# Transposing the first branch's h and three groups of q, k by VectorE and DRAM instead of TensorE

## The chip, the cores and the metric

The program runs on one core of one Trainium2 chip. The metric is the device time of one execution in microseconds (us), the median of three runs. A core has TensorE (matrix products and, with an identity matrix as one operand, transposes; results go to the PSUM banks), VectorE (DVE), ScalarE (ACT), GpSimd (POOL), and SyncE (SP), which here issues nearly all DMAs. Each engine takes its own instructions in order and waits on semaphores for the others. All DMAs run on the same 16 DMA engines.

## The reference

A layer for 512 tokens with 1024 channels: a feed-forward block, then two branches that read the same normalized tokens u, then a second feed-forward block. All is float32. What matters here is the middle:

```python
z = u @ w_mix + b_mix                       # q_m,k_m,v_m,o_m, i,f gates, q_f,k_f,v_f, f_f, g_a,g_b
h_m = mlstm_chunkwise(q_m, k_m, v_m, i_m, f_m)                  # 4 heads of 256 channels
y_a = sigmoid(o_m) * rms_norm(h_m, mlstm_norm_g)                # the first branch, 512 x 1024
y_b = forgetting_attention(q_f, k_f, v_f, f_f, q_g, k_g)        # 16 heads of 64, q and k rms-normed
merged = sigmoid(g_a) * (y_a @ w_branch_a) + sigmoid(g_b) * (y_b @ w_branch_b)
x = x + g2 * (merged @ w_out)               # g2 etc. come from silu(c) @ w_ada + b_ada
```

The inputs' gains and biases are larger than usual, so products are taken in three float32r passes (below).

## The kernel before, in words

Every large product is split: an operand is kept as a high part in float32r and the rest as a low part, and each product of 128 x 128 weights with 512 columns is three matmuls (`mm3`, lines 127 to 129). A weight chunk arrives in a buffer `raw` (three of them, `raw`, line 92), ScalarE rounds it to `wh` (line 102), VectorE subtracts to get `wl` (line 104), four buffers each.

The stage that the change touches lies between about 470 us and 830 us of the span. Tokens lie in four blocks of 128 (`tb`). A value can lie token-major (partition = token) or channel-major (partition = channel).

- `mlstm_h(h)` makes the first branch's output of one of four heads token-major: for each token block, products into PSUM, a division into `hn` (line 1107), squares on ScalarE (line 1109); then a reciprocal root over the four blocks, four multiplications by VectorE (line 1115) and four stores to a DRAM tile `h_d` (line 1116). Two token blocks share one buffer of the tag `bc`, four buffers, which the broadcast rows of later heads use too.
- `fox_qkv(g)` makes q and k of four attention heads at a time, g = 0 to 3, token-major: 256 channels of q and 256 of k in one tile `tk` per token block (tag `tok`, four buffers). When the last chunk is in, `done` adds the bias (line 1127), then squares, sums, a reciprocal root and a multiplication by it (line 1147). Then it makes v.
- `fox_t(p)` turns the q and k of one pair of heads channel-major: four TensorE transposes of 128 x 128 for q and four for k (line 1202) into a PSUM bank, from which ScalarE (lines 1207 and 1211) and VectorE (line 1209) write the gained high and low parts `fq`, `fk` and `klz`. There are eight pairs, two to a group.
- `fox_s`, `fox_p`, `fox_o` are the scores, the softmax with the transposes of its result (line 1259), and the product with v, for one head each. `fox_s` loads a row A of `A_d` spread over the partitions (line 1219).
- `y_a(m)`, m = 0 to 7, is the output gate of 128 channels: a product with `w_mix`, a tanh (line 1309), a load of h from `h_d` as `ht` (line 1311, tag `tok`), four TensorE transposes (line 1314), a scaling by ScalarE into `ya` (line 1316) and a product by VectorE (line 1317). From m = 4 on each half of it also takes one step of `ada_row`: 128 rows of `w_ada` are loaded through `raw` and added up, scaled, by VectorE (line 304).

`run` writes the order: the attention's heads go through n = 0 to 17, and between their parts `advance(fill, k)` takes k steps of a generator that holds half chunks of the next group's `fox_qkv`, some gates (`gate`, whose result is stored at line 1335), and, from n = 12, `y_a`. `fox_t(1)` stands at n = 1, `fox_t(2)` at n = 3, and so on to `fox_t(6)` and `fox_t(7)` at n = 11. This written order is a priority. When the program is built, a planner in the framework takes, engine by engine, the first instruction in that order whose operands and buffers are free by its own modelled durations, so that an instruction may move ahead of others: the loads of four `ht` leave SP together, as soon as buffers of `tok` come free. On the chip each engine's order is then fixed.

Of the kernel before, what the change touches and what calls it, by code (L numbers as in the profile page):

```python
# [11 lines left out]
F32 = mybir.dt.float32  # L12
# [35 lines left out]
class Layer:  # L48
    def __init__(self, tc, es, A, out, dbg=None):
        self.tc, self.nc, self.es, self.A, self.out = tc, tc.nc, es, A, out  # L50
        self.dbg = dbg or {}
        pool = lambda name, **k: es.enter_context(tc.tile_pool(name=name, **k))
        self.cp = pool("const", bufs=1)
        self.up = pool("u", bufs=1)
        self.xp = pool("x", bufs=1)
        self.wp = pool("w", bufs=4)
        self.sp = pool("small", bufs=4)
        self.pg = pool("pg", bufs=4, space=PSUM)
        self.pt = pool("pt", bufs=4, space=PSUM)
# [3 lines left out]
        self.due = []  # L63
        self.free = self.pin = lambda i: i

# [223 lines left out]
    def ada_row(self, v, new, new_row, bank):  # L289
# [800 lines left out]
    def mlstm_h(self, h, ip):  # L1090
        nc, sp = self.nc, self.sp
        (Wh, Wl), (vh, vl) = self.W[h], self.vt[h]
        ss = sp.tile([P, NT], F32, name=self.nm("hs"), tag="hs", bufs=2)
        hs = []
        for tb in range(NT):
            if tb % 2 == 0:
                h2 = ip.tile([P, 2, 256], F32, name=self.nm("hn"), tag="bc", bufs=4)
            ps = self.tbank()
            for sb in range(tb + 1):
# [14 lines left out]
        for tb in range(NT):  # L1114
            nc.vector.tensor_scalar(hs[tb], hs[tb], r[:, tb:tb + 1], None, op0=MUL)
            nc.sync.dma_start(self.h_d[tb * P:(tb + 1) * P, h * 256:(h + 1) * 256], hs[tb])


    def fox_qkv(self, g, ip):
# [25 lines left out]
        for tb in range(NT):  # L1145
            t3 = tok[tb].rearrange("p (h d) -> p h d", h=8)
            nc.vector.tensor_tensor(t3, t3, r[:, tb * 8:(tb + 1) * 8].unsqueeze(2).to_broadcast([P, 8, 64]), op=MUL)
        if g == 3:
            self.fx[g] = tok, self.fx[g]
            return  # L1150
# [14 lines left out]
        def mkv(ch):  # L1165
# [7 lines left out]
            return make  # L1173
        self.fx[g] = (tok, vts[0])
        if len(gs) > 1:
            self.fx[3] = vts[1]
        if g:
# [6 lines left out]
    def fox_t(self, p, ap):  # L1184
# [13 lines left out]
        for i, R in ((0, R_FQ), (1, R_FK)):  # L1198
            c = i * 256 + pr * P
            b = self.tbank()  # L1200
            for tb in range(NT):
                nc.tensor.transpose(b[:, tb * P:(tb + 1) * P], tok[tb][:, c:c + P], self.ident)
            gc = self.colA[:, R + p:R + p + 1]
# [90 lines left out]


    def y_a(self, m, ap, ip):
        nc = self.nc
        def step():
            if m >= NK // 2:
                self.tick()  # L1300
# [10 lines left out]
        nc.sync.dma_start(ht, self.h_d[:, m * P:(m + 1) * P].rearrange("(b p) n -> p b n", p=P))  # L1311
        b = self.tbank()
        for tb in range(NT):
            nc.tensor.transpose(b[:, tb * P:(tb + 1) * P], ht[:, tb, :], self.ident)
        ya = ap.tile([P, T], F32, name=self.nm("ya"), tag="qk", bufs=16)
        nc.scalar.activation(ya, b, AF.Copy, scale=self.hmg[:, m:m + 1])
        nc.vector.scalar_tensor_tensor(ya, th, 1.0, ya, op0=ADD, op1=MUL)
        self.ya[m] = ya
        step()
        yield  # L1320
# [42 lines left out]
    def run(self):  # L1363
# [3 lines left out]
        self.h_d = self.dp.tile([T, D], F32, name="h_d")  # L1367
        self.v0_d = [self.dp.tile([P, 256], F32, name=f"v0_d{tb}") for tb in range(NT)]
        self.g_d = [self.dp.tile([P, T], F32, name=f"g_d{i}") for i in range(2 * NK)]

# [145 lines left out]
        with tc.tile_pool(name="att", bufs=1) as ip:  # L1516
# [17 lines left out]
            self.vt, self.W, self.fx, self.qkt, self.S = [None] * 4, {}, {}, {}, {}  # L1534
            def advance(gen, n):
                for _ in range(n):
                    next(gen, None)
            advance(self.v_mlstm(0, ip, ip), 99)
# [13 lines left out]
            for n in range(18):  # L1552
# [18 lines left out]
            advance(fill, 99)  # L1571
            for m in range(NK):
                self.dump(f"ya_{m}", self.ya[m])
# [94 lines left out]
```

## Time and profile before

| | |
|---|---|
| median of three runs | 1321.18 us (1319.3 to 1321.39) |
| the profiled execution, its own time | 1319.86 us |
| its span | 1318.1 us, 17796 instructions |
| granted TensorE clock | 1.00 of full speed |
| TensorE busy | 1303.3 us, 99% |
| VectorE busy | 953.4 us, 72% |
| ScalarE busy | 630.3 us, 48% |
| DMA | 254.18 MB in 204488 packets |

The profiled execution takes 1.8 us more than its span, and lies 1.3 us below the median. "PE" is TensorE's matmuls (transposes among them), "PEld" its weight loads. Matmuls overlap, so that the duration of one is longer than its pitch; a row of several, xN, of the chain view gives the time that they take on the path. An entry "A <- B" in a list of waits says that A waited and B ended the wait.

### The profile page before, as it was taken

How to read it: one execution, taken by the hardware profiler on the slowest of the kernel's cores; microseconds unless marked ns; L12 is line 12 of the kernel's file. 1: busy time of each engine (PE TensorE's matmuls, PEld its weight loads, DVE VectorE, ACT ScalarE, POOL GpSimd, SP SyncE). 2: the span in 40 equal slices, each digit the busy share in tenths (PEclk: the TensorE clock that was granted, in tenths of full speed). 3: DMA queues.
4: the chain of work that ended last, by engine and by line, in shares of the span. 5: the costliest groups of instructions: out<-in, count | busy, mean ns of one | idle time of the engine just before them, and what ended most of it. 6: DMA issues, size and time to landing. Idle time of an engine off the chain costs nothing.

```text
span 1318.1 us, 17796 instructions
## 1 busy us (share of the span) xinstructions
PE 1303.3 (99%) x6345; PEld 1092.2 (83%) x6345; DVE 953.4 (72%) x1735; ACT 630.3 (48%) x1056; POOL 36.9 (3%) x57
## 2 busy tenths in 40 slices
PE   7999999999999999999999999999999999999998
PEld 6788888888899888888888788878898888888887
DVE  6877777578788687887887778777567557635787
ACT  5623232355476555566566666334372223223642
POOL 1000000000010101000000000003000000000000
PEclk9999999999999999999999999999999999999999
DMA  9998978465845434533343536777539767634574
GB/s 287 278 316 291 326 265 278 149 198 166 299 120 145 117 104 130 155 106 113 89 121 76 171 98 194 215 255 234 185 104 325 255 232 278 220 104 133 171 263 149
DMA packets 204488, 254.18 MB, mean 193 GB/s; under 512 B 15008, under 2 KB 146752, under 8 KB 204400
## 3 DMA queue, kind: packets, MB, share of 16 engines
q1 hardware_dynamic: 204016, 252.98, 60.1%
q8 instruction: 50, 0.82, 0.3%
q14 instruction: 38, 0.31, 0.1%
q0 software_dynamic: 320, 0.06, 0.0%
q10 hardware_dynamic: 64, 0.02, 0.0%
HBM read 217.28 MB, written 35.72 MB: 192 GB/s over the span
## 4 chain that ended last, share of the span: by engine, by line
PE 86%; DMA 4%; DVE 4%; ACT 3%; SPq 1%; issue 1%; DVEq 0%; ACTq 0%
PE g L129 22%; PE g L127 22%; PE g L128 22%; PE t L127 4%; PE t L129 4%; PE t L128 4%; DMA raw<-in_w_branch_a_dram 2%; PE g L909 1%; PE t L1289 1%; PE t L1259 1%; DMA raw<-in_w_ada_dram 1%; PE t L1230 1%; DVE wl L104 1%; PE t L1231 1%; DMA raw<-in_w_branch_b_dram 1%
## 5 line engine op out<-in xcount | busy, mean ns | idle before, releaser
L102 ACT ACTIVATE wh<-raw 128x1024 fp32r<-128x1024 f32 (+2 forms) x246 | 249.2, 1017 | 378.0 <-PE g L128 118.5
L104 DVE TENSOR_TENSOR wl<-raw,wh 128x1024 fp32r<-128x1024 f32 (+2 forms) x246 | 287.2, 1170 | 163.9 <-ACT wh L102 141.9
L127 PE MATMUL g<-uh,wh 128*128 128x512 f32 (+1 forms) x880 | 341.0, 387 | 0.0
L128 PE MATMUL g<-ul,wh 128*128 128x512 f32 (+1 forms) x880 | 339.5, 386 | 0.4 <-DVE ul L268 0.4
L129 PE MATMUL g<-uh,wl 128*128 128x512 f32 (+1 forms) x880 | 339.6, 386 | 0.0
L129 PEld LDWEIGHTS g<-uh,wl 128*128 128x128 f32 x880 | 165.3, 188 | 33.6
L128 PEld LDWEIGHTS g<-ul,wh 128*128 128x128 f32 x880 | 165.4, 188 | 33.2 <-DVE ul L268 0.6
L127 PEld LDWEIGHTS g<-uh,wh 128*128 128x128 f32 x880 | 165.3, 188 | 32.6 <-issue 0.6
L304 DVE SCALAR_TENSOR_TENSOR acc<-raw,ccol,acc 128x512 f32<-128x512 f32 (+1 forms) x70 | 66.8, 975 | 45.0 <-DMA raw<-in_w_ada_dram 44.9
L127 PE MATMUL g<-wh,uh 128*128 128x512 f32 (+1 forms) x256 | 97.4, 381 | 0.0
L129 PE MATMUL g<-wh,ul 128*128 128x512 f32 (+1 forms) x256 | 96.7, 378 | 0.0
L128 PE MATMUL g<-wl,uh 128*128 128x512 f32 (+1 forms) x256 | 96.4, 377 | 0.0
L127 PE MATMUL t<-wh,A 128*128 128x512 f32 x176 | 68.6, 390 | 0.0
L128 PE MATMUL t<-wl,A 128*128 128x512 f32 x176 | 68.5, 389 | 0.0
L129 PEld LDWEIGHTS g<-wh,ul 128*128 128x128 f32 x256 | 48.2, 188 | 9.1
L127 PEld LDWEIGHTS g<-wh,uh 128*128 128x128 f32 x256 | 48.2, 188 | 8.7 <-DVE tk L1127 0.5
L128 PEld LDWEIGHTS g<-wl,uh 128*128 128x128 f32 x256 | 48.2, 188 | 8.3
L129 PE MATMUL g<-yh,wl 128*128 128x512 f32 x128 | 50.1, 391 | 0.8 <-DVE wl L104 0.8
L127 PE MATMUL g<-yh,wh 128*128 128x512 f32 x128 | 49.9, 390 | 0.0
L128 PE MATMUL g<-yl,wh 128*128 128x512 f32 x128 | 49.8, 389 | 0.0
L420 ACT ACTIVATE A<-E 128x768 fp32r<-128x768 f32 x22 | 18.6, 846 | 55.5 <-DVE E L419 55.5
L1241 ACT ACTIVATE S<-S,mn 128x128 f32<-128x128 f32 (+1 forms) x64 | 35.5, 556 | 16.1 <-DVE mn L1233 9.9
(360 smaller groups left out, 2240.8 us busy)
## 6 DMA issues: line engine op xcount, KB each, us to landing
raw<-in_ffn_w_in_dram SPq DMA_DIRECT2D x82, 512.0 KB, 4.5
raw<-in_w_ada_dram SPq DMA_DIRECT2D x56, 512.0 KB, 5.6
raw<-in_w_mix_dram SPq DMA_DIRECT2D x46, 512.0 KB, 4.3
sa<-in_ffn_w_out_dram SPq DMA_DIRECT2D x22, 512.0 KB, 6.3
sb<-in_ffn_w_out_dram SPq DMA_DIRECT2D x44, 256.0 KB, 6.6
ws<-sa SPq DMA_DIRECT2D x22, 512.0 KB, 4.1
ws<-sb SPq DMA_DIRECT2D x44, 256.0 KB, 4.8
raw<-ws SPq DMA_DIRECT2D x44, 256.0 KB, 3.6
```

Of the source, the lines that this page charges most:

```text
L102: nc.scalar.activation(hi, src, AF.Copy)
L104: self.last_lo = nc.vector.tensor_tensor(lo, src, hi, op=SUB)
L127: pin(mm(ps, lh, rh, start=start, stop=False))
L128: pin(mm(ps, lh, rl, start=False, stop=False))
L129: self.last_mm = pin(mm(ps, ll, rh, start=False, stop=stop))
L304: nc.vector.scalar_tensor_tensor(a, r[:, s], c, a, op0=MUL, op1=ADD)
L420: nc.scalar.activation(A1[:, 0:3, :], E[:, 0:3, :], AF.Copy)
L909: pin(nc.tensor.matmul(acc_ps[b], (wl if p == 1 else wh)[:, b % 2, s], self.ul[k] if p == 2 else self.uh[k], start=k == 0 and p == 0, stop ...
L1230: nc.tensor.matmul(ps[:, :w], q[:, s], k[:, :w], start=True, stop=False)
L1231: nc.tensor.matmul(ps[:, :w], q[:, s], kl[:, :w], start=False, stop=True)
L1241: nc.scalar.activation(S[:, ws], S[:, ws], AF.Exp, scale=-1.0, bias=m, accum_out=sm[:, qb:qb + 1])
L1259: tr = lambda b, c, qb, kb: nc.tensor.transpose(b[:, c:c + P], S[:, P_OFF[qb] + kb * P:P_OFF[qb] + (kb + 1) * P], self.ident)
```

## The change

- In `mlstm_h` the last scaling moves from VectorE to ScalarE. After two blocks VectorE transposes the pair's tile of 128 x 512 in place; this instruction transposes each square of 32 x 32 by itself. One DMA per pair then stores it to `h_d`, as a *post*: it is written into the program one step of `advance` later.
- In `fox_qkv` for g = 1, 2, 3 VectorE transposes each `tk` tile in the same way, and a post stores it to a new DRAM tile `t_d[g]`. A second post, three steps later, (`bring`) loads four channel-major tiles of 128 x 512, in the order of the pairs, into the same four buffers.
- `blocks` is the load that completes a transpose: four DMAs per tile, each for 32 partitions, that take 16 squares of 32 x 32 to their places, in runs of 32 elements (128 bytes).
- `fox_t` for g = 1 to 3 reads these tiles where it read a PSUM bank. Group 0 keeps the TensorE transposes.
- `y_a` loads `ht` with `blocks`, one m ahead, and ScalarE scales it straight from there. VectorE's last product is written one step later.
- `ada_row` in `y_a` uses two buffers of its own (`ring`, in a buffer of the tag `vm`) where it used `raw`.

```diff
+    def post(self, steps, f):
+        self.posts.append([steps, f])
+    def advance(self, gen, n):
+        for _ in range(n):
+            next(gen, None)
+            for p in self.posts[:]:
+                p[0] -= 1
+                if p[0] < 0:
+                    self.posts.remove(p)
+                    p[1]()
...
-            r = self.raw([P, D], [(lambda t: t, A["w_ada"][0, k * P:(k + 1) * P, v * D:(v + 1) * D])])
+            src = A["w_ada"][0, k * P:(k + 1) * P, v * D:(v + 1) * D]
+            if self.ring is None:
+                r = self.raw([P, D], [(lambda t: t, src)])
+            else:
+                r = self.ring[:, k % 2, :]
+                nc.sync.dma_start(r, src)
...
-            nc.vector.tensor_scalar(hs[tb], hs[tb], r[:, tb:tb + 1], None, op0=MUL)
-            nc.sync.dma_start(self.h_d[tb * P:(tb + 1) * P, h * 256:(h + 1) * 256], hs[tb])
+            nc.scalar.activation(hs[tb], hs[tb], AF.Copy, scale=r[:, tb:tb + 1])
+            if tb % 2:
+                t = h2s[tb // 2].rearrange("p b n -> p (b n)")
+                nc.vector.transpose(t, t)
+                self.post(1, lambda t=t, b=tb - 1: nc.sync.dma_start(
+                    self.h_d[b * P:(b + 2) * P, h * 256:(h + 1) * 256].rearrange("(b p) n -> p b n", p=P),
+                    t.rearrange("p (b n) -> p b n", b=2)))
+
+    def blocks(self, t, src):
+        for j in range(4):
+            self.nc.sync.dma_start(t[32 * j:32 * j + 32, :].rearrange("a (t b) -> a t b", b=32),
+                                   src[:, 32 * j:32 * j + 32].rearrange("(t a) b -> a t b", a=32))
...
+            if g:
+                t = tok[tb]
+                nc.vector.transpose(t, t)
+                self.post(1, lambda t=t, tb=tb: nc.sync.dma_start(self.t_d[g][tb * P:(tb + 1) * P, :], t))
+        def bring():
+            qk = [ip.tile([P, T], F32, name=self.nm("fT"), tag="tok", bufs=4) for _ in range(4)]
+            for n in (0, 2, 1, 3):
+                self.blocks(qk[n], self.t_d[g][:, n * P:(n + 1) * P])
+            self.fx[g][0] = qk
+        if g:
+            self.post(3, bring)
...
-            c = i * 256 + pr * P
-            b = self.tbank()
-            for tb in range(NT):
-                nc.tensor.transpose(b[:, tb * P:(tb + 1) * P], tok[tb][:, c:c + P], self.ident)
+            if g:
+                b = tok[2 * i + pr]
+            else:
+                b = self.tbank()
+                c = i * 256 + pr * P
+                for tb in range(NT):
+                    nc.tensor.transpose(b[:, tb * P:(tb + 1) * P], tok[tb][:, c:c + P], self.ident)
...
+    def ht_load(self, m, ip):
+        t = ip.tile([P, T], F32, name=self.nm("ht"), tag="tok", bufs=4)
+        self.blocks(t, self.h_d[:, m * P:(m + 1) * P])
+        self.ht.append(t)
...
+        if m == 0:
+            self.ht = []
+            self.ht_load(0, ip)
         self.gemm_stat(ps, w, 0, T, range(0, 4))
         step()
         yield
+        if m + 1 < NK:
+            self.ht_load(m + 1, ip)
         self.gemm_stat(ps, w, 0, T, range(4, 8))
+        ht = self.ht[m]
         th = self.tmp(ip, "th")
         nc.scalar.activation(th, ps, AF.Tanh, scale=0.5, bias=self.hom[:, m:m + 1])
-        ht = ip.tile([P, NT, P], F32, name=self.nm("ht"), tag="tok", bufs=4)
-        nc.sync.dma_start(ht, self.h_d[:, m * P:(m + 1) * P].rearrange("(b p) n -> p b n", p=P))
-        b = self.tbank()
-        for tb in range(NT):
-            nc.tensor.transpose(b[:, tb * P:(tb + 1) * P], ht[:, tb, :], self.ident)
         ya = ap.tile([P, T], F32, name=self.nm("ya"), tag="qk", bufs=16)
-        nc.scalar.activation(ya, b, AF.Copy, scale=self.hmg[:, m:m + 1])
-        nc.vector.scalar_tensor_tensor(ya, th, 1.0, ya, op0=ADD, op1=MUL)
+        nc.scalar.activation(ya, ht, AF.Copy, scale=self.hmg[:, m:m + 1])
+        self.post(1, lambda: nc.vector.scalar_tensor_tensor(ya, th, 1.0, ya, op0=ADD, op1=MUL))
```

More of the change, by code (lines that the diff above doesn't have):

```diff
@@ L63, in __init__ @@
         self.due = []
+        self.posts = []
+        self.ring = None
         self.free = self.pin = lambda i: i
@@ L1173, in mkv @@
             return make
-        self.fx[g] = (tok, vts[0])
-        if len(gs) > 1:
-            self.fx[3] = vts[1]
+        for i, vt in zip(gs, vts):
+            self.fx[i] = [tok, vt]
         if g:
@@ L1368, in run @@
         self.v0_d = [self.dp.tile([P, 256], F32, name=f"v0_d{tb}") for tb in range(NT)]
+        self.t_d = [self.dp.tile([T, 512], F32, name=f"t_d{g}") for g in range(4)]
         self.g_d = [self.dp.tile([P, T], F32, name=f"g_d{i}") for i in range(2 * NK)]
@@ L1534, in run @@
             self.vt, self.W, self.fx, self.qkt, self.S = [None] * 4, {}, {}, {}, {}
-            def advance(gen, n):
-                for _ in range(n):
-                    next(gen, None)
+            advance = self.advance
             advance(self.v_mlstm(0, ip, ip), 99)
@@ L1571, in run @@
             advance(fill, 99)
+            self.ring = None
             for m in range(NK):
```

6 lines of the change are left out of this document (4 added, 2 removed).

## The prediction

> **What bounds the kernel now.** I read the page first (busy time, the 40 slices, the chain), then busy time by stretches of the stage that is touched, then the chain of waits in that stage.
>
> ```profile
> PE 1303.3 (99%) x6345; PEld 1092.2 (83%) x6345; DVE 953.4 (72%) x1735; ACT 630.3 (48%) x1056; POOL 36.9 (3%) x57
> PE   7999999999999999999999999999999999999998
> PE 86%; DMA 4%; DVE 4%; ACT 3%; SPq 1%; issue 1%; DVEq 0%; ACTq 0%
> ```
>
> TensorE is busy in every slice and is 86% of the chain that ended last. Work taken from TensorE is therefore worth its time, as long as the other engines keep feeding it. The stretches, with columns TensorE, its weight loads, VectorE, ScalarE, GpSimd, granted clock, DMA share and GB/s:
>
> ```profile
> 520.00:560.00 40.00, 39.60 (x211) 33.95 (x210) 33.65 (x113) 21.32 (x47) 0.00 (x0) 1.00 0.51 152
> 560.00:600.00 40.00, 39.82 (x244) 35.51 (x243) 35.38 (x102) 25.58 (x57) 0.00 (x0) 1.00 0.39 114
> 640.00:680.00 40.00, 39.87 (x200) 32.95 (x200) 37.58 (x100) 27.37 (x58) 0.00 (x0) 1.00 0.38 112
> 720.00:760.00 40.00, 39.28 (x200) 32.30 (x199) 30.68 (x81) 27.47 (x57) 0.00 (x0) 1.00 0.55 162
> 790.00:822.00 32.00, 32.00 (x170) 27.19 (x169) 29.68 (x58) 19.16 (x37) 0.00 (x0) 1.00 0.64 187
> 470.00:830.00 360.00, 358.44 (x1874) 303.20 (x1873) 287.19 (x763) 217.95 (x463) 3.77 (x4) 1.00 0.42 123
> ```
>
> The reader is to see three things: over the whole stage TensorE lacks 1.56 us of 360; the clock is full; VectorE is next, at 287 of 360 on average and 37.58 of 40 in 640 to 680.
>
> **The change part by part.** *TensorE loses 80 transposes.* `fox_t` of pairs 2 to 7 has 6 x 8 = 48, `y_a` has 8 x 4 = 32. Two rows by line, and two of the chain in order of time:
>
> ```profile
> L1202 PE MATMUL t<-ident,tk 128*128 128x128 f32 x64 | 8.1, 272 | 0.0
> L1314 PE MATMUL t<-ident,ht 128*128 128x128 f32 x32 | 4.8, 271 | 0.0
> 634.05 0.87 PE t L1202 x8
> 769.27 0.44 PE t L1314 x4
> ```
>
> The 272 ns of one overlap with its neighbours. What a transpose takes on the path is the chain's 0.87 / 8 = 0.109 us (0.44 / 4 = 0.11 in `y_a`). So 80 x 0.109 = **8.7 us** go. The busy column bounds it from above: 48 x 8.1 / 64 + 4.8 = 10.9 us. These rows lie on the chain, which is why I count them whole.
>
> *VectorE and ScalarE.* These rows price the rest:
>
> ```profile
> L1147 DVE TENSOR_TENSOR tk<-tk,rq 128x512 f32<-128x512 f32 x16 | 10.2, 684 | 0.0
> L1115 DVE TENSOR_SCALAR hn<-hn,rq 128x256 f32<-128x256 f32 x16 | 5.6, 412 | 0.1
> L1109 ACT ACTIVATE hj<-hn 128x256 f32<-128x256 f32 x16 | 6.6, 414 | 8.4 <-DVE d L1105 4.8 <-DVE hn L1107 3.2
> L1209 DVE SCALAR_TENSOR_TENSOR klz<-t,colA,fk 64x512 fp32r<-64x512 f32 x16 | 12.0, 750 | 2.3 <-ACT fk L1207 1.8
> L1317 DVE SCALAR_TENSOR_TENSOR ya<-th,ya 128x512 f32<-128x512 f32 x8 | 5.5, 689 | 1.9 <-ACT ya L1316 1.7
> ```
>
> VectorE gains 8 transposes for h and 12 for q, k, each of 128 x 512. No row shows that instruction. Its lower end is twice the fastest kind of 256 columns, 2 x 5.6 / 16 = 0.70, about the 0.684 of line 1147, which moves as many elements within SBUF; its upper end is two passes, 2 x 0.684 = 1.37. I take 0.68, the row of the same size: 20 x 0.68 = 13.6 us. VectorE loses line 1115 (5.6 us), and 24 products of line 1209 read SBUF in place of PSUM: 0.750 against 0.689 in line 1317, so 1.5 us less. Net +6.5 us in 287.
>
> The Trainium skill speaks for the upper end: in "VectorE: DVE Perf Modes", The three transpose paths, its table gives 311 ns for a 128 x 128 bf16 transpose by VectorE. No run here shows it; by it 512 columns would be estimated at 4 x 0.311 = 1.24 us, and the sum at 24.9 us in place of 13.6.
>
> Where does VectorE's surplus meet a full stretch? Each group adds 4 x 0.68 - 8 x 0.06 = 2.2 us. In 640 to 680 that makes 39.8 us, while TensorE needs only 39.1 there (eight transposes fewer): **0.7 us** come out late. In 560 to 600 it makes 37.6 of 40, in 720 to 760 32.9: covered. For h, 520 to 560 has 33.65 plus 4 x 0.68 less about half of line 1115: covered, and nobody waits for h before `y_a`. ScalarE takes over 16 x 0.414 = 6.6 us at 21.32 of 40; covered by its idle time.
>
> *DMAs.* Twenty tiles x 4 `blocks` DMAs, plus 12 stores to `t_d` and 8 to `h_d`, less 16 stores and 8 loads: 76 more issues on SP's queue. One `blocks` DMA has 512 packets of 128 bytes, 32 per engine. The first four rows below are the loads of `ht` (512 packets of 512 bytes, issue in ns, and landing), and stores of 256 and 128 KB. The last four are two stretches of 1.0 us (377.55 to 378.55) and 4.2 us (746 to 750.2): all packets, then the queue's packets, MB and share of 16 engines.
>
> ```profile
> L1311 SPq DMA_DIRECT2D ht<-h_d x8: 359/378/513, 744.8 to 786.7; - x8
> DMA to landing us min/median/max: 2.8/2.8/2.8
> g_d<-tg SPq DMA_DIRECT2D x14, 256.0 KB, 2.0
> h_d<-hn SPq DMA_DIRECT2D x16, 128.0 KB, 1.8
> DMA packets 828, 0.03 MB, mean 31 GB/s; under 512 B 828, under 2 KB 828, under 8 KB 828
> q1 hardware_dynamic: 828, 0.03, 50.7%
> DMA packets 2183, 1.29 MB, mean 306 GB/s; under 512 B 76, under 2 KB 2124, under 8 KB 2183
> q1 hardware_dynamic: 2183, 1.29, 101.8%
> ```
>
> A packet of well under 512 bytes held an engine 0.507 x 1.0 x 16 / 828 = 9.8 ns, one of mostly 512 bytes 1.018 x 4.2 x 16 / 2183 = 31 ns. So a `blocks` DMA takes 32 x 9.8 to 32 x 31 ns = 0.31 to 1.0 us of all engines, against 0.378 us to issue: its pitch is 0.38 to 1.0 us. A group's sixteen take 6 to 16 us, and at most 16 of the 40 us of a stretch in which the DMA engines stand at 0.31 to 0.55. Bandwidth is covered. I take the pitch near the lower end, 0.5, since 128 bytes lie nearer the small packets.
>
> The Trainium skill says the contrary of short runs: "DMA: Bandwidth & Descriptors", Specifications, wants 512 B or more for line rate and speaks of read-modify-write below that. In this trace the packets under 512 bytes are shorter, 9.8 ns against 31, though per byte they are dearer; by that rule a run of 128 bytes would cost no less than one of 512, the upper end above, 16 us a group.
>
> *When q and k arrive.* Before, nothing but TensorE lay between line 1147 and `fox_t`. Now a store, SP, and a load do. VectorE's last scalings of the groups, and the first readers:
>
> ```profile
> 586.38 2.48 DVE L1147 TENSOR_TENSOR tk<-tk,rq 128x512 f32<-128x512 f32 x4
> 650.15 2.50 DVE L1147 TENSOR_TENSOR tk<-tk,rq 128x512 f32<-128x512 f32 x4
> 722.61 2.49 DVE L1147 TENSOR_TENSOR tk<-tk,rq 128x512 f32<-128x512 f32 x4
> 603.95 0.68 ACT L1207 ACTIVATE fq<-t,colA 64x512 fp32r<-64x512 f32 x1
> 671.79 0.67 ACT L1207 ACTIVATE fq<-t,colA 64x512 fp32r<-64x512 f32 x1
> 744.29 0.67 ACT L1207 ACTIVATE fq<-t,colA 64x512 fp32r<-64x512 f32 x1
> ```
>
> Group 1: scaled at 588.9, transposed 4 x 0.68 later at 591.6, stored at 593.6, eight loads of the first pair at 0.38 to 1.0 us each, landed 2.8 us on: 599.4 to 604.4, for 604.0. Groups 2 and 3: 663.2 to 668.2 for 671.8, and 735.6 to 740.6 for 744.3. By the slow pitch group 1 is **0.4 us** late and the others have 3.6 us to spare. The second pairs are wanted some 30 us later.
>
> *The waits on SP, and the buffers.* The loads wait for the stores. Behind them on SP stand weight loads, the rows A and gate stores; SP is held like this already (the rows of SP from 560 to 830 us, the other two from 560 to 745):
>
> ```profile
> SPq L92 <- DVE wl L104: 83.7, 27, 7.4
> SPq L1335 <- ACT tg L1333: 39.2, 9, 13.0
> DVE tk L1127 <- PE t L1202: 9.7, 3, 4.4
> PEld g L127 <- DVE tk L1127: 0.7, 3, 0.3
> ```
>
> Holds of up to 13.0 us cost TensorE almost nothing today, so six more us of issuing per group do not either. The `tok` buffers are wanted by the next group's line 1127, which waits for the last transposes (9.7 us in three waits); TensorE pays 0.7 us for it. Now the four ScalarE and VectorE instructions of each half of `fox_t` free them, later by some 3 us, but those no longer wait for TensorE: I count zero. Freed PSUM banks: zero, there is only 1.56 us to win.
>
> *`ring`, `ht` a step ahead, the late product.* `y_a` stands between 760 and 822, where TensorE is at 32.00 of 32.00 in the second half; nothing to win, so zero. What covers a late row is TensorE's queue of prepared weights; what is given back if that fails is small, since `ya` is read only after the stage.
>
> **The sum.** -8.7 + 0.7 + 0.4 = -7.6 us, against the profiled execution's 1319.86: 1312.3. That execution lies 1.3 us below the median of 1321.2, so a median of **1313.6 us**, 0.6% faster. Less than 0.2%, 2.6 us, can hardly be told from no change here.
>
> **The rivals.** *Late tiles (slower).* Place: SP ahead of `bring`. If SP sits in a wait when the loads could go, the first pair's tiles come late, ScalarE's fixed order stands at line 1207, and softmax and weights behind it stop TensorE. Holds of the mean size, 39.2 / 9 = 4.4 us, would make the groups 4.8 + 0.8 + 0.8 = 6.4 us late, and leave -8.7 + 0.7 + 6.4 = -1.6: 1319.6, no change. It decides from 5 us per hold; at 8 us it is 8.4 + 4.4 + 4.4 = 17.2 us late, +9.2: 1330. For it: three such chains in a row, and a longest hold of 13.0. Against it: the planner sets a load on SP only where its store is done by the model, so a wait is the model's error alone, and the steps of a post push a load's priority back, not its time.
>
> *VectorE's transpose costs 1.37 us.* Then 5.0 us more per group: 42.6 against 39.1 in 640 to 680, 40.4 against 40 in 560 to 600: 3.9 us late, sum -8.7 + 3.9 + 0.4 = -4.4: 1316.8. For it: nothing in the trace excludes it. Against it: all rows of 512 columns in one pass lie at 0.68 to 0.69.
>
> The Trainium skill's table of transposes (the section named above) leads here, with its 1.24 us.
>
> *More than the transposes.* VectorE's waits at line 1127 go and TensorE's 1.56 us with them: -10.3, 1311.
>
> *Nothing moves.* The taken work only opens gaps, because heads end when their softmax does: 1321. Against it stands a TensorE with generators of products to fill in.
>
> **How the numbers follow.** Forecast 0.50 (1310 to 1317 by itself); late tiles by much 0.20, by the mean hold 0.08; dear transpose 0.10; more 0.08; nothing 0.04. Faster 0.50 + 0.10 + 0.08 = 0.68; within 0.2% 0.08 + 0.04 = 0.12; slower 0.20. The range runs from 1309, below the larger gain, to 1324, which leaves out the large delays alone.
>
> **What would show it.** Right: 80 fewer matmuls, TensorE's busy time down by 8 to 11 us, lines 1207 and 1209 of pairs 2, 4 and 6 within a us or two of their place; the new VectorE rows near 0.68 us; loads from `t_d` at 0.4 to 0.6 us each. Wrong: ScalarE or VectorE waiting for a DMA of `fT`, a TensorE slice below 9 between 590 and 760, SP's waits behind `t_d` stores of 5 us or more, or VectorE full in 640 to 680.

## The result, and the profile after

The changed kernel takes 1326.24 us (median of 6 runs, 1324.94 to 1327.32) against 1320.71 beside it: ratio 1.0046, 95% interval 1.0035 to 1.0056. It is slower by 5.5 us, where 1313.6, 7.6 us less, was forecast. Two slow executions, 2657.2 us among those of the kernel before and 4627.64 us among the four of `e14_gd_act_ring_pool` below, are left out of every median and difference here. Its profiled execution has a span of 1324.2 us, against 1318.1. From the page after, busy time and the slices of TensorE:

```profile
PE 1302.0 (98%) x6265; PEld 1089.5 (82%) x6265; DVE 959.3 (72%) x1739; ACT 638.2 (48%) x1072; POOL 38.2 (3%) x57
PE   8999999999999999999999898999999999999998
```

The 80 transposes are gone (6345 to 6265), and yet TensorE's busy time falls by 1.3 us only, since at a lower clock each matmul is busy for longer (the distance of two starts is 0.43 us in place of 0.23, see the first place). Slices 23 and 25 drop to 8, between 728 and 828 us. By stretches, after (columns as in the prediction):

```profile
640.00:680.00 40.00, 40.00 (x199) 33.80 (x198) 37.18 (x110) 26.79 (x61) 0.00 (x0) 1.00 0.47 110
720.00:760.00 40.00, 36.54 (x185) 30.39 (x183) 24.56 (x67) 26.92 (x55) 0.00 (x0) 0.99 0.48 100
760.00:800.00 40.00, 38.74 (x182) 31.51 (x183) 31.12 (x86) 24.02 (x57) 0.00 (x0) 0.93 0.63 133
800.00:840.00 40.00, 34.64 (x146) 27.57 (x145) 29.50 (x44) 19.47 (x30) 0.00 (x0) 0.91 0.61 177
```

The same two last stretches before:

```profile
760.00:800.00 40.00, 40.00 (x221) 34.30 (x221) 32.43 (x93) 25.79 (x63) 0.00 (x0) 1.00 0.41 121
800.00:840.00 40.00, 40.00 (x193) 33.45 (x193) 33.04 (x49) 21.49 (x36) 0.00 (x0) 1.00 0.63 189
```

Up to 680 us nothing is lost: VectorE is not full in 640 to 680, and TensorE is. In 680 to 720 TensorE idles 0.65 us (39.35 of 40.00, before 39.98). From 720 to 840 TensorE is idle for 10.1 us (3.46 + 1.26 + 5.36) and has a lower clock; that is the stage of the output gates, `y_a`. The parts that concern the groups came as costed; after, VectorE's transposes (h, then q and k), and the loads by `blocks` with their issue in ns (those of `fT` land 2.5 us after it, median of the sixteen of group 1):

```profile
L1138 DVE STREAM_TRANSPOSE hn<-hn x8: 668/704/711, 489.6 to 548.8; 128x512 f32<-128x512 f32 x8
L1181 DVE STREAM_TRANSPOSE tk<-tk x12: 669/689/709, 588.0 to 716.2; 128x512 f32<-128x512 f32 x12
L1146 SPq DMA_DIRECT2D fT<-t_d x48: 303/487/1069, 594.3 to 728.4; - x48
L1146 SPq DMA_DIRECT2D ht<-h_d x32: 371/487/1752, 740.1 to 800.8; - x32
```

And the first reader of group 1, which was at 603.95; those of groups 2 and 3, which were at 671.79 and 744.29, now stand at 655.60 and 723.18:

```profile
599.53 0.71 ACT L1250 ACTIVATE fq<-fT,colA 64x512 fp32r<-64x512 f32 x1
```

**The first place, near 757 us.** SP's queue after, every entry from 725 to 754 us:

```profile
725.72 3.14 SPq L1146 DMA_DIRECT2D fT<-t_d  x6
728.96 11.01 SPq L1386 DMA_DIRECT2D g_d<-tg  x3
740.08 0.37 SPq L1146 DMA_DIRECT2D ht<-h_d  x1
749.78 0.32 SPq L1386 DMA_DIRECT2D g_d<-tg  x1
750.17 3.66 SPq L1146 DMA_DIRECT2D ht<-h_d  x7
753.88 0.49 SPq L106 DMA_DIRECT2D raw<-in_w_mix_dram  x1
```

The load of `w_mix` before this one left at 710.35. From 728.96 on SP stands at the gate's stores `g_d` (line 1386), which wait for a tanh, and then issues seven loads of `ht` ahead of the weights. A long stretch without weights is no loss by itself: before, none of `w_mix` leaves SP from 738.35 to 766.64, and TensorE is full from 760 on. After, ScalarE has nothing left to round: its rounding at 759.31 has waited 2.50 us for the load of 753.88. SP's largest wait of 718 to 760 us (total, times, longest), after, and the same stores in the same window before:

```profile
SPq L1386 <- ACT tg L1384: 20.0, 4, 9.3
```

```profile
SPq L1335 <- ACT tg L1333: 9.9, 4, 5.7
```

TensorE pays when it gets there (after; start, duration, and in brackets the idle time before):

```profile
760.42 0.80 PE L141 MATMUL g<-uh,wh 128*128 128x512 f32 x1 [3.12 <-ACT wh L116]
...
762.36 0.79 PE L143 MATMUL g<-uh,wl 128*128 128x512 f32 x1 [0.72 <-DVE wl L118]
762.95 0.63 PE L141 MATMUL g<-uh,wh 128*128 128x512 f32 x1
763.38 0.63 PE L142 MATMUL g<-ul,wh 128*128 128x512 f32 x1
```

It idles 3.12 + 0.72 us, and its matmuls then follow each other in 0.43 us (762.95 to 763.38) until about 765, against 0.23 later (766.04 to 766.27).

**The second place, 804 to 824 us.** ScalarE after, all of 813 to 817 us, and TensorE's three largest waits of the stretch:

```profile
813.78 0.69 ACT L1365 ACTIVATE th<-g,hom 128x512 f32<-128x512 f32 x1 [7.42 <-PE g L143]
814.49 0.59 ACT L1335 ACTIVATE yt<-t 64x512 f32<-64x512 f32 x1
815.10 0.72 ACT L1367 ACTIVATE ya<-ht,hmg 128x512 f32<-128x512 f32 x1
815.73 1.99 ACT L116 ACTIVATE wh<-raw 128x1024 fp32r<-128x1024 f32 x2
```

```profile
806.72 0.50 PE L1332 MATMUL t<-Pl,fvt 128*128 128x512 f32 x1 [1.36 <-DVE Pl L1301]
...
816.82 0.80 PE L141 MATMUL g<-uh,wh 128*128 128x512 f32 x1 [2.74 <-ACT wh L116]
...
818.55 0.80 PE L143 MATMUL g<-uh,wl 128*128 128x512 f32 x1 [0.51 <-DVE wl L118]
```

ScalarE, idle for 7.42 us, stands at the tanh of one product, which waits for TensorE to end that product; only behind it does its fixed order round the weights of the next. So TensorE has no prepared weights when the product ends. Before, the rounding stands ahead of the tanh in this stretch:

```profile
803.18 1.06 ACT L102 ACTIVATE wh<-raw 128x1024 fp32r<-128x1024 f32 x1 [2.16 <-DMA raw<-in_w_mix_dram]
804.15 0.67 ACT L1309 ACTIVATE th<-g,hom 128x512 f32<-128x512 f32 x1
...
810.64 1.06 ACT L102 ACTIVATE wh<-raw 128x1024 fp32r<-128x1024 f32 x1 [1.47 <-DMA raw<-in_w_mix_dram]
...
812.90 0.69 ACT L1309 ACTIVATE th<-g,hom 128x512 f32<-128x512 f32 x1
```

Earlier in `y_a` it stands behind the tanh in both kernels (before at 770.69 behind 769.55, after at 769.86 behind 769.27), and TensorE loses nothing there. The wait of 1.36 us is another one: VectorE makes two products of a row (804.67, 1.39 us) ahead of the `Pl` that TensorE wants. SP stands in the same stretch as well, at a row's load that waits for VectorE (745 to 830 us, after; total, times, longest):

```profile
SPq L316 <- DVE acc L323: 29.1, 3, 17.7
```

Whether SP's wait or ScalarE's order makes the second gap is what the later experiments tell apart.

### The profile page after: what moved, and what is told of

Read it like the earlier page. It is cut to its first block, busy times and chain, and to the rows that moved or that the text cites. A ratio compares the mean times of both kernels' runs of the same rounds, so it can differ in the third digit from the quotient of the medians.

```text
span 1324.2 us, 17789 instructions
## 1 busy us (share of the span) xinstructions
PE 1302.0 (98%) x6265; PEld 1089.5 (82%) x6265; DVE 959.3 (72%) x1739; ACT 638.2 (48%) x1072; POOL 38.2 (3%) x57
## 4 chain that ended last, share of the span: by engine, by line
PE 86%; DVE 5%; DMA 3%; ACT 3%; issue 1%; SPq 1%; ACTq 0%; DVEq 0%
PE g L143 23%; PE g L142 23%; PE g L141 22%; PE t L141 4%; PE t L142 4%; PE t L143 4%; PE g L928 1%; DMA raw<-in_ffn_w_out_dram 1%; PE t L1332 1%; DVE wl L118 1%; PE t L1302 1%; PE t L1273 1%; ACT wh L116 1%; PE t L1274 1%; PE t L928 1%
## 5 line engine op out<-in xcount | busy, mean ns | idle before, releaser
L323 DVE SCALAR_TENSOR_TENSOR acc<-raw,ccol,acc 128x1024 f32<-128x1024 f32 (+1 forms) x56 | 56.9, 1032 | 37.2 <-DMA raw<-in_w_ada_dram 37.0
```

Of the source, the lines that this page charges most:

```text
L323: nc.vector.scalar_tensor_tensor(a, r[:, s], c, a, op0=MUL, op1=ADD)
```

## The experiments

**Parts of the change.** `e1_qk` has only the part of q and k; h, `y_a` and the rows are as before.

```diff
-            nc.scalar.activation(hs[tb], hs[tb], AF.Copy, scale=r[:, tb:tb + 1])
...
+            nc.vector.tensor_scalar(hs[tb], hs[tb], r[:, tb:tb + 1], None, op0=MUL)
+            nc.sync.dma_start(self.h_d[tb * P:(tb + 1) * P, h * 256:(h + 1) * 256], hs[tb])
...
-            self.ht_load(m + 1, ip)
...
+        for tb in range(NT):
+            nc.tensor.transpose(b[:, tb * P:(tb + 1) * P], ht[:, tb, :], self.ident)
```

> q and k of groups 1 to 3 by VectorE and DRAM as in the change; h, the output gates and the rows of w_ada as before. Theory A (all the loss sits in the output gates, at 755 to 824 us, and the part with q and k is sound): 48 transposes x 0.109 us = 5.2 us less than before, about 1316 us, and TensorE without a gap over 1 us after 740. Theory B (q and k that arrive otherwise push the attention's end into the output gates): slower than before or equal, 1321 to 1326, with the gap near 757 still there.

1317.08 us, ratio 0.9976 (0.9966 to 0.9985): 3.6 us won of 48 x 0.109 = 5.2. One gap over 1 us is left, 2.18 us near 773 us behind VectorE's softmax, which theory A had excluded. `e2_h` is the rest: h, `y_a` and `ring` as in the change, q and k by TensorE.

```diff
...
-        if g:
-            self.post(3, bring)
...
```

> The counterpart: h, the output gates and the two buffers for rows as in the change, q and k by TensorE as before. Theory A: the gaps of the changed kernel near 757 and 804 to 818 come with it, about 1326 + 5 = 1331 us. Theory B: no such gaps, 32 x 0.109 = 3.5 us less than before, about 1317 us.

1322.57 us, ratio 1.0012 (1.0003 to 1.0022), between the two theories' 1331 and 1317. A loss lies in the part of h and `y_a`, though it saves 32 transposes. The two parts add up to -3.6 + 1.9 = -1.7 us, the change gives +5.5: together they cost 7 us that neither has alone. `e9_qk_ring` is `e1_qk` with the rows in `ring`:

```diff
+                if self.ring is None:
+                    self.ring = ip.tile([P, 2, D], F32, name="ring", tag="vm", bufs=3)
```

> q and k as in the change, h as before, and the rows of w_ada in two buffers of their own as in the change. The two buffers were worth 1331.95 - 1326.24 = 5.7 us beside the short-run loads of h. If they help whatever loads h, 1312 to 1314 us against the 1317.08 of the same without them; if they only made good what those loads took, 1316 to 1318 us.

1314.12 us, ratio 0.9951 (0.9936 to 0.9966). `e3_noring` is the change with the rows through `raw`:

```diff
-                if self.ring is None:
-                    self.ring = ip.tile([P, 2, D], F32, name="ring", tag="vm", bufs=3)
```

> The change, with the rows of w_ada in the output gates through the three weight buffers as before. Theory A1 (SP stands 17.7 us in front of a row's load whose buffer VectorE has not read, with weight loads behind it): the second gap (804 to 824) goes, 7 to 9 us less than the change, about 1318 us; the first gap, near 757, stays. Theory A2 (the short-run loads of h hold the DMA engines and SP): both gaps stay, 1326 us.

1331.95 us, ratio 1.0088 (1.0073 to 1.0103): both theories missed. So the two buffers are no cause; they save 5.7 us here, 3.0 from `e1_qk` to `e9_qk_ring`. `e6_nopost` writes the product of `y_a` at its place:

```diff
-        self.post(1, lambda: nc.vector.scalar_tensor_tensor(ya, th, 1.0, ya, op0=ADD, op1=MUL))
+        nc.vector.scalar_tensor_tensor(ya, th, 1.0, ya, op0=ADD, op1=MUL)
```

> The change, with the last product of y_a written at its place and not a step later. Theory S: the post is no cause by itself; only where the planner puts the products of the rows on VectorE may move by it, so the time stays at 1323 to 1328 as long as SP's hold at a row's load stays, and is 1316 to 1320 if that hold shrinks under 10 us. Rival L (the late product is what delays VectorE's rows): the hold goes and the time is under 1320 with the rows spread over 770 to 800.

1328.02 us, ratio 1.0054 (1.0039 to 1.0069), which overlaps the change's interval: the late product is no cause either. What is left of `y_a` are the loads of `ht`.

**The loads of `ht`.** `e5_ht1dma` loads each `ht` with one DMA in runs of 512 bytes, and so leaves out putting the squares in their places:

```diff
-        self.blocks(t, self.h_d[:, m * P:(m + 1) * P])
+        self.nc.sync.dma_start(t.rearrange("p (b n) -> p b n", b=NT), self.h_d[:, m * P:(m + 1) * P].rearrange("(b p) n -> p b n", p=P))
```

> The change, but each tile of h is loaded for the output gates by one DMA of 512 runs of 512 bytes in place of four of 512 runs of 128 bytes. The squares then are not put in their places, so the first branch is wrong; all else runs the same. Theory A2: 24 issues and three quarters of the packets less, the first gap (3.1 us near 757 and the half clock after it) goes, and with it the delay that leads to the second: 8 to 13 us less than the change, 1313 to 1318 us. Theory A1: SP still stands in front of the row's load, the second gap stays, 1322 to 1326 us.

1312.06 us, ratio 0.9936 (0.9921 to 0.9951): 8.65 us below before, near the forecast price of 80 transposes. Is it the number of issues, or the short runs? `e8_ht1short` issues one DMA with runs of 128 bytes (2048 packets), `e7_ht4long` four DMAs of 32 partitions with runs of 512 bytes; both leave out putting the squares in their places.

```diff
-        self.blocks(t, self.h_d[:, m * P:(m + 1) * P])
+        b = m % 4
+        self.nc.sync.dma_start(t.rearrange("p (c n) -> p c n", n=32),
+                               self.h_d[b * P:(b + 1) * P, :].rearrange("p (c n) -> p c n", n=64)[:, :, m // 4 * 32:m // 4 * 32 + 32])
```

```diff
-        self.blocks(t, self.h_d[:, m * P:(m + 1) * P])
+        for j in range(4):
+            r = slice(32 * j, 32 * j + 32)
+            self.nc.sync.dma_start(t[r, :].rearrange("p (b n) -> p b n", b=NT),
+                                   self.h_d[:, m * P:(m + 1) * P].rearrange("(b p) n -> p b n", p=P)[r])
```

> The counterpart: one DMA for each tile of h, of 2048 runs of 128 bytes (from other places of h, so the first branch is wrong). If it is the packets, the loss stays: 1322 to 1326 us, DMA engines at 0.9 and more from 750 to 780. If it is the issues, 1311 to 1314 us.

> The change with each tile of h still loaded by four DMAs of 32 partitions, but in runs of 512 bytes (128 packets each, the same bytes). The squares are not put in their places, so the first branch is wrong. If it is the issues (four at 0.49 us each on SP, ahead of weight loads), the loss stays: 1322 to 1326 us, the gap near 757 within a us of the change's. If it is the number of packets (13824 of 128 bytes in 30 us), it goes: 1311 to 1314 us, as with one DMA of long runs (1312.06).

1313.75 us (0.9949, 0.9934 to 0.9964) and 1312.47 us (0.9934, 0.9916 to 0.9952). Neither alone costs more than 2 us over `e5_ht1dma`, so both explanations fall; in `e8_ht1short` the DMA engines even stand at 0.90 in 760 to 800. But in each kernel the planner makes another order, which these runs do not hold still: in all three TensorE is at 40.00 of 40.00 in 800 to 840, and near 805 us the rounding stands ahead of the tanh, as before (804.46 and 805.43 in `e5_ht1dma`, 806.48 and 807.45 in `e8_ht1short`, 800.33 and 807.35 in `e7_ht4long`). `e10_store` moves the short runs to the stores of h (`h_d` channel-major, eight short-run DMAs per pair, each `ht` one long load):

```diff
...
+                    for j in range(4):
+                        for i in range(2):
+                            o = (b + i) * P + 32 * j
+                            nc.sync.dma_start(
+                                self.h_d[h * 256:(h + 1) * 256, o:o + 32].rearrange("(c a) n -> a c n", a=32),
+                                t[32 * j:32 * j + 32, i * 256:(i + 1) * 256].rearrange("a (c n) -> a c n", n=32))
...
-        self.blocks(t, self.h_d[:, m * P:(m + 1) * P])
+        self.nc.sync.dma_start(t, self.h_d[m * P:(m + 1) * P, :])
```

> The change with the short runs of h moved from the load to the store: eight DMAs of 32 partitions per pair of token blocks write h channel-major, between 490 and 550 us, where the DMA engines stand at 0.4 to 0.5 and nothing waits for h; each tile for the output gates is then one load of 128 rows of 2 KB. The full computation. If the time of the short runs in the output gates is the cause, this has neither: 1311 to 1313 us. If short runs hurt wherever they lie (64 more issues in front of the rows M and A and of weights at 490 to 560), a new gap there, 1315 to 1322 us.

1323.83 us, ratio 1.0020 (1.0009 to 1.0031). From 800 us on TensorE is full again (40.00 of 40.00 in 800 to 840), and the loss comes right behind the place where the stores went (`e10_store`; 39.82 before):

```profile
560.00:600.00 40.00, 34.51 (x201) 29.76 (x199) 28.63 (x91) 20.77 (x49) 0.00 (x0) 0.92 0.43 126
```

`e13_ht_pool` issues the loads of `ht` from GpSimd's queue:

```diff
-        self.blocks(t, self.h_d[:, m * P:(m + 1) * P])
+        for j in range(4):
+            self.nc.gpsimd.dma_start(t[32 * j:32 * j + 32, :].rearrange("a (t b) -> a t b", b=32),
+                                     self.h_d[:, m * P + 32 * j:m * P + 32 * j + 32].rearrange("(t a) b -> a t b", a=32))
```

> The change, with the four DMAs of each tile of h issued from GpSimd's queue, which is idle, and all else on SP. SP is rid of 32 issues, the gate stores still hold it until about 750. If SP's queue behind the stores is what delays the weights (theory C), the first weight load goes out at 750 and not 754, and the second gap goes: 1312 to 1317 us. If the short runs fill the DMA engines (theory D): 1322 us or more.

1317.85 us, ratio 0.9974 (0.9963 to 0.9985): 8.4 us better than the change, 0.85 above theory C's range. TensorE is at 40.00 in 800 to 840, where the rounding stands ahead of the tanh again, and at 35.86 in 760 to 800. So what the loads do to SP and to the order around it counts.

**The first place.** `e11_gd_act` issues the gate's stores from ScalarE's queue, behind the tanh that they wait for:

```diff
-            nc.sync.dma_start(self.g_d[8 * i + m], th)
+            nc.scalar.dma_start(self.g_d[8 * i + m], th)
```

> The change, with the gates' stores issued from ScalarE's own queue behind the tanh that makes them, not from SP. In the change SP stood 20.0 us between 718 and 760 in front of these stores, and the weight load that TensorE lacked at 757 went out at 753.88. Theory C (the loss begins with SP held in front of the gate stores, and the short-run loads of h only use up what is left of the cover): the weight load goes out before 745, both gaps go, 1311 to 1315 us. Theory D (the DMA engines, full from 755 to 780, are enough by themselves): at least half of the loss stays, 1320 us or more.

1321.49 us, ratio 1.0004 (0.9993 to 1.0014): 4.75 us better than the change. SP and the stretches of `e11_gd_act`:

```profile
743.04 0.49 SPq L106 DMA_DIRECT2D raw<-in_w_mix_dram  x1
```

```profile
720.00:760.00 40.00, 38.60 (x194) 32.01 (x193) 28.12 (x83) 28.16 (x62) 0.00 (x0) 1.00 0.64 137
...
800.00:840.00 40.00, 36.16 (x139) 28.73 (x140) 29.73 (x42) 16.50 (x25) 0.00 (x0) 0.87 0.64 191
```

The weights leave at 743.04 in place of 753.88, TensorE has 2.1 us more work in 720 to 760, and the half clock there is gone. So theory C holds for the first place; the second is untouched, with the same waits of 1.36, 2.74 and 0.51 us, and the time stays above 1320. `e12_best` is `e9_qk_ring` with the same edit:

```diff
-            nc.sync.dma_start(self.g_d[8 * i + m], th)
+            nc.scalar.dma_start(self.g_d[8 * i + m], th)
```

> q and k as in the change, h as before, two buffers for rows, gate stores from ScalarE's queue. By theory C the 1.4 us still lost near 770 in the same kernel with stores from SP (1314.12 us) go in part: 1312 to 1314 us. If ScalarE's time for 14 issues counts: 1314 to 1317 us.

1312.89 us, ratio 0.9939 (0.9923 to 0.9956): the best kernel of this study that does the whole layer, 8.3 us below before, with h and `y_a` left to TensorE. That is 3.1 more than its 48 transposes were priced at; 0.8 of it is TensorE's idle time in 520 to 840 us (0.75 against 1.57 before), and no run takes the rest apart.

**The second place: SP's hold?** `e15_ring_pool` issues the rows' loads from GpSimd's queue, `e14_gd_act_ring_pool` does so beside the edit of `e11_gd_act`.

```diff
                 r = self.ring[:, k % 2, :]
-                nc.sync.dma_start(r, src)
+                nc.gpsimd.dma_start(r, src)
```

> The change, with the gate's stores (g_d) issued from ScalarE's queue and the rows' loads into ring issued from GpSimd's queue. Theory S (SP stands at a row's load that waits 17.7 us for VectorE's product of the row before, with weight loads behind it): the load now waits on a queue that nobody else uses here, the gap of TensorE near 808 to 818 goes with its half clock, and with the first gap gone too the time is 1312 to 1315 (1321.5 with the stores alone moved; 1312.1 with each ht in one DMA). Rival V (the late product itself, or transfers that are slow in this stretch, stop TensorE): the gap stays, 1319 to 1323.

> The change, with only the rows' loads into ring issued from GpSimd's queue; the gate's stores stay on SP. Theory S: the first gap (near 757, SP at the gate's stores) stays with its half clock, the second goes: 1316 to 1320, some 6 to 9 below the change. Rival V: 1324 to 1328. By S the two moves should add up with e14: the change's loss over 1312 is split between them.

1313.20 us (0.9948, 0.9929 to 0.9968) and 1318.93 us (0.9985, 0.9976 to 0.9994). In `e15_ring_pool` the second place loses 1.0 us, at full clock:

```profile
800.00:840.00 40.00, 39.00 (x179) 31.86 (x178) 30.98 (x44) 20.70 (x31) 0.53 (x1) 1.00 0.54 157
```

Against the change that is -4.8 for the stores, -7.3 for the rows' loads, -13.0 for both: two causes that about add up, and with both gone the kernel is at its forecast. But the planner also made another order in these two: VectorE's products of the rows come earlier, the wait of 1.36 us is gone, and the rounding stands right behind the tanh (810.87 behind 810.28 in `e15_ring_pool`; TensorE waits 0.46 us for it), where the change has two more instructions between (815.73 behind 813.78). `e16_ring4` takes the hold away in another way, with four buffers for the rows; ScalarE's order in the stretch is that of the change.

```diff
-                r = self.ring[:, k % 2, :]
+                r = self.ring[k // 2 % 2][:, k % 2, :]
...
-                    self.ring = ip.tile([P, 2, D], F32, name="ring", tag="vm", bufs=3)
+                    self.ring = [ip.tile([P, 2, D], F32, name=n, tag="vm", bufs=3) for n in ("ring", "ring2")]
```

> The change with four buffers for the rows in the output gates in place of two; all loads stay on SP, the gate's stores too, and VectorE's order through the first rows is that of the change (the products of the third row behind the output of a head and a product of y_a). Theory S (SP's standing at the third and fourth row's load is the cause of the second gap): these loads no longer wait, the next w_mix load leaves SP some 17 us earlier than 806.5, the gap of 804 to 820 goes or shrinks to under 2 us, the first gap stays: 1317 to 1321, as with the rows' loads on GpSimd's queue (1318.9). Rival O (VectorE's late row products cost the time themselves, and only the new order of e15 helped): 1324 to 1328.

1328.22 us, ratio 1.0050 (1.0032 to 1.0069): no gain. My theory of SP's hold fell here, and the rows of `e16_ring4` say why: SP's longest wait at a row is 9.7 us in place of 17.7; the weights in question leave SP at 789.34; the DMA engines are idle in 795 to 800, so they are in; and ScalarE rounds them at 817.67 (the first of the two there), behind a tanh, as in the change. ScalarE has stood idle for 8.78 us ahead of that tanh, with these weights in. The waits of TensorE are those of the change, 1.36, 2.74 and 0.51 us.

```profile
789.34 0.40 SPq L106 DMA_DIRECT2D raw<-in_w_mix_dram  x1
```

```profile
795.00:800.00 5.00, 4.92 (x29) 3.98 (x28) 4.52 (x6) 3.59 (x9) 0.00 (x0) 1.00 0.01 3
```

```profile
815.71 0.69 ACT L1365 ACTIVATE th<-g,hom 128x512 f32<-128x512 f32 x1 [8.78 <-PE g L143]
...
817.67 1.99 ACT L116 ACTIVATE wh<-raw 128x1024 fp32r<-128x1024 f32 x2
```

**Or ScalarE's order?** `e17_w_ahead` asks for the weights of the next product half a product earlier. `e19_wh_first` adds only that a tanh may not stand ahead of that rounding, and `e21_wh_first_gd_act` adds the edit of `e11_gd_act` to it.

```diff
...
+            self.wn = self.w_stat(self.A["w_mix"][0], OM + (m + 1) * P)
             self.ht_load(m + 1, ip)
...
```

```diff
...
-        nc.scalar.activation(th, ps, AF.Tanh, scale=0.5, bias=self.hom[:, m:m + 1])
+        with self.tc.issue_after(self.last_hi.ins):
+            nc.scalar.activation(th, ps, AF.Tanh, scale=0.5, bias=self.hom[:, m:m + 1])
```

> The change, with the weights of the next product of y_a asked for half a product earlier (load, wh and wl). ScalarE's order still has the rounding of the next weights (wh, L116) behind the tanh of this product in most of the eight steps. Theory P (what stops TensorE at 804 to 820 is this order on ScalarE: the tanh waits for the end of a product, and only behind it the weights of the next are rounded): the second gap stays, 1322 to 1327. Rival S (the load leaves SP too late): the earlier loads help, under 1321.

> As e17_w_ahead, and the tanh of a product of y_a may stand on ScalarE only behind the rounding of the next weights (now directly ahead of each tanh from the second on). SP, the rows' loads, ht and the gate's stores as in e17. Theory P: the gaps at 804 and at 814 go or shrink to under 1 us each, the first gap near 757 stays: 1317 to 1321. Rival S: no gain over e17, within 2 us of it, or slower, since the tanh may now wait for a load.

> As e19_wh_first, and the gate's stores issued from ScalarE's queue. Theory P: both gaps go, 1312 to 1316, with the rows' loads still on SP. Rival S: 1318 or more.

1323.88 us (1.0026, 1.0016 to 1.0036), 1317.92 us (0.9982, 0.9973 to 0.9991), 1313.72 us (0.9948, 0.9933 to 0.9963). The 2.4 us of `e17_w_ahead` over the change lie at the first place (TensorE 38.40 in 720 to 760, against 36.54); the second stays. ScalarE near 805 us in `e17_w_ahead` (rounding `wh` behind the tanh `th`) and its stretch:

```profile
806.07 0.69 ACT L1366 ACTIVATE th<-g,hom 128x512 f32<-128x512 f32 x1 [3.96 <-PE g L143]
807.89 1.06 ACT L116 ACTIVATE wh<-raw 128x1024 fp32r<-128x1024 f32 x1
```

```profile
800.00:840.00 40.00, 33.98 (x132) 26.66 (x131) 29.47 (x43) 17.46 (x27) 0.00 (x0) 0.87 0.64 184
```

and in `e19_wh_first`:

```profile
802.64 1.06 ACT L116 ACTIVATE wh<-raw 128x1024 fp32r<-128x1024 f32 x1
804.44 0.69 ACT L1367 ACTIVATE th<-g,hom 128x512 f32<-128x512 f32 x1 [0.74 <-PE g L143]
...
811.62 0.69 ACT L1367 ACTIVATE th<-g,hom 128x512 f32<-128x512 f32 x1 [4.63 <-PE g L143]
812.33 1.06 ACT L116 ACTIVATE wh<-raw 128x1024 fp32r<-128x1024 f32 x1
```

```profile
800.00:840.00 40.00, 35.91 (x157) 28.19 (x156) 32.02 (x46) 18.62 (x27) 0.00 (x0) 1.00 0.77 222
```

The half clock goes and 6.0 us with it. A gap at 811 to 815 stays, where a rounding stands behind a tanh once more (the constraint does not reach the first weights of the next stage), so "under 1 us each" was too much. With SP's first hold gone as well, 1313.72 is the forecast again, with the rows' loads still on SP. So the order on ScalarE is shown as the cause at the second place, with two open ends. It costs only where TensorE has nothing else to do, since `e15_ring_pool` keeps the rounding behind the tanh and loses little. And the wait of 1.36 us behind VectorE's row products is gone in `e15_ring_pool`, and in `e17_w_ahead` already, so that the 6.0 us hold none of it; what it costs in the change no run shows by itself. Why the planner puts the rounding behind the tanh with 32 loads of `ht` by `blocks` on SP, and ahead of it with 8 loads, with 32 of long runs, or with the 32 on GpSimd's queue, is its own model's doing, and no run here looks into it.

## Why the prediction was wrong

- *Right in the main: 80 x 0.109 = 8.7 us.* `e5_ht1dma` is 8.65 us below before; `e14_gd_act_ring_pool` and `e21_wh_first_gd_act` 7.8 and 6.7, with part of the gates' gaps left. That the first meets 8.7 to 0.05 is luck: TensorE idles 2.7 us in 680 to 800 in it, against 0.7 before.
- *Right: VectorE's price.* 0.68 was taken, 0.70 and 0.69 were measured. The dear transpose of the rivals is out, and with it the estimate from the Trainium skill, "VectorE: DVE Perf Modes", The three transpose paths. By its 311 ns for 128 x 128 in bf16 a transpose of 512 columns would be estimated at 1.24 us; the rows above say 0.70 for float32, so the estimate is too high. ("All rows of 512 columns in one pass lie at 0.68 to 0.69" overlooked the 0.750 of line 1209, to no effect.)
- *Too careful: 0.7 + 0.4 us late.* The 0.4 was worked out with the slow pitch of 1.0 us, though 0.5 had been chosen, by which nothing is late. TensorE is at 40.00 in 640 to 680, VectorE at 37.18 and not 39.8, and the first readers came 4, 16 and 21 us earlier than before. The loads' issue takes 0.487 us (median), and six in a row take 3.14 us, a pitch of 0.52. The heaviest rival, late tiles in `bring`, did not happen.
- *Wrong: "nothing to win, so zero" for `ring`, `ht` a step ahead and the late product, with "what covers a late row is TensorE's queue of prepared weights".* I asked what a late `ya` could cost, and its reader is indeed far away. I did not ask what stands behind these instructions on their engines. With the edits the planner's order in the second half of `y_a` has the rounding of the next weights behind the tanh, and the cover that I named, prepared weights, is what failed: some 6 us (`e17_w_ahead` to `e19_wh_first`), 7.3 by `e15_ring_pool`, which takes the 1.36 us behind VectorE with it. The term was also wrong in sign for `ring`, which alone saves 3.0 to 5.7 us.
- *Wrong: "holds of up to 13.0 us cost TensorE almost nothing today, so six more us of issuing per group do not either".* The holds at the gate's stores doubled (9.9 to 20.0 us) and eight loads of `ht` came to stand between them and the weights: 4.75 us (`e11_gd_act`).
- The sum with these terms: -8.7 + 7.3 + 4.8 = +3.4, measured +5.5. Of the rest, 0.9 of the 8.7 is not won in `e14_gd_act_ring_pool` (7.8), and its two moves together are worth 0.9 more than apart (13.0 against 12.1); the last 0.3 is the kernel before, 1320.71 beside the change and 1320.97 beside `e14_gd_act_ring_pool`.

The forecast's own sign of failure, a TensorE slice below 9 between 590 and 760, did show, but for another reason than the one that it stood for. A rival with ScalarE's order standing still was there, at `fox_t`; the same mechanism struck at `y_a`.

## What to carry to other kernels

An edit that nobody waits for is free only if what stands behind it in the same in-order queue isn't waited for either: list, for SP and ScalarE, what follows each moved or added instruction, up to the next weights. A full engine with 40.00 of 40.00 says that its cover holds now, and a plan that is made anew can take the cover away: look at whether the rounding of the next weights still stands ahead of the instruction that waits for this product. When a gain is missing, remove each suspected hold by itself and together, and hold the order still in one of the runs; here a removal that worked, the other queue, would have told a wrong story without one that did not, the four buffers.

## What the runs showed of the hardware

- A short stop of TensorE can cost more than itself, since the granted clock may fall behind it. After, the five microseconds with the waits of 3.12 and 0.72 us have a clock of 0.50 behind them; in `e17_w_ahead` waits of 1.76 and 1.03 us with some matmuls between do the same:

```profile
760.00:765.00 5.00, 3.86 (x8) 2.65 (x9) 3.97 (x16) 2.73 (x9) 0.00 (x0) 0.50 1.00 182
```

```profile
810.00:815.00 5.00, 4.15 (x10) 3.29 (x11) 2.12 (x3) 0.00 (x0) 0.00 (x0) 0.50 1.00 302
```

  Not every such stop does: in `e19_wh_first` waits of 1.85 and 1.38 us, at 811.6 to 815.6, leave the clock at 1.00.

```profile
810.00:815.00 5.00, 2.32 (x10) 1.26 (x8) 2.65 (x4) 1.74 (x2) 0.00 (x0) 1.00 1.01 338
```

  The Trainium skill, "TensorE: Matmul & The Clock Gate", What's actually happening, gives an idle window of about 3.4 us for the fall. The 3.12 us of the change are near that size; `e17_w_ahead` shows the fall behind two waits that are each shorter, and `e19_wh_first` none behind two of like length, so no length of a wait decides it in these runs.
- Packets of mostly 128 bytes. In 594 to 603.5 us, after, the sixteen loads of group 1 move (all packets, then the queue's packets, MB and share):

```profile
DMA packets 7287, 1.16 MB, mean 122 GB/s; under 512 B 7028, under 2 KB 7284, under 8 KB 7284
...
q1 hardware_dynamic: 7284, 1.13, 70.6%
```

  One held an engine 0.706 x 9.5 x 16 / 7284 = 14.7 ns, against 31 ns for one of mostly 512 bytes in the prediction's rows. The Trainium skill's words on runs below 512 bytes ("DMA: Bandwidth & Descriptors", Specifications) hold per byte here, not per packet: a short packet was the cheaper one. Neither the short runs (`e8_ht1short`) nor the number of loads (`e7_ht4long`) cost more than 1.7 us alone; what the loads cost came from where they stood on SP's queue and from the order that the planner made around them.
